# Ten of sixteen 256-column groups of the second block's first FFN product as seven products of half blocks

## The chip, the core and the metric

The kernel runs on one core of a Trainium2 chip. The metric is the device time of one execution in microseconds (us). One execution is also taken with the hardware profiler; its rows are what this text reads. Engines are named as in the profile: PE (TensorE, matmuls), PEld (its weight loads), DVE (VectorE), ACT (ScalarE), POOL (GpSimd) and SP (which only issues transfers here).

## What is computed

Two blocks of a transformer, each with two layers, on 512 tokens of 1024 features in float32. The change touches only the feed-forward part of the second block, twice (two layers):

```python
D_FF_2 = 4 * D_MODEL            # 4096, with D_MODEL = 1024 and 512 tokens

def second_block(x, ...):
    for l in range(DEPTH):      # DEPTH = 2
        ...                     # mixer: pooling and sparse attention
        h = rms_norm_2(x, g_pre_ffn[l])
        f = jnp.square(jax.nn.relu(h @ w_ff1[l])) @ w_ff2[l]
        x = x + rms_norm_2(f, g_post_ffn[l])
```

The first product is `h @ w_ff1[l]`: 512 x 1024 by 1024 x 4096.

## The kernel before, in words

**Float32 by three products.** Every weight and every activation that goes into a large product is split into a high part (type fp32r, tiles `wh`, `hh`) and the rest (`wl`, `hl`). `mm3` issues three matmuls, high by high, high by low, low by high, which add up in PSUM. ACT makes the high part of a weight tile of 128 x 1024 (L212) and DVE subtracts it for the low part (L214). The third matmul of `mm3` is the first that reads `wl`.

**Weights.** `specs` lists all weight tiles in the order of use. `prefetch_raw` issues their loads on SP into two buffers `wr`; `prefetch` splits them; `weights()` hands the next one out and keeps two split tiles (two buffers of `wh` and `wl`) ahead. `place_next` names another tile as the place of a coming split.

**The first FFN product, `ffn2`.** The hidden features come in eight groups g of 512 columns. A group takes four weight tiles (256 rows by 512 columns each), and of each tile 24 matmuls with 512 moving columns (tokens): 96 matmuls, into four PSUM tiles `mm`. The sums over the eight row blocks are kept with features on the partitions, four tiles of 128 x 512. When one is done, ACT writes its relu into `hq<g>` (L1631) and DVE squares it there (L1632). The normalisation's gain per feature is in `hh` and `hl` already; its factor per token is applied after the second product. In the last layer `last_tokens` (32 transposes of `x` on PE, eight copies on ACT) is woven into group 1. Then `out_ffn` or, in the last layer, `out_last` makes the second product.

**Half blocks elsewhere.** `gemm_feat_halves` already runs group 0 in halves of 256 tokens: its matmuls have 256 moving columns, with a weight load of 128 x 128 for each as everywhere.

**Order.** The program is written as generators; a scheduler then places the instructions on the engines, each of which runs its own queue in order.

Of the kernel before, what the change touches and what calls it, by code (L numbers as in the profile page):

```python
# [9 lines left out]
F32 = mybir.dt.float32  # L10
# [6 lines left out]
P = 128  # L17
# [74 lines left out]
class Net:  # L92
# [36 lines left out]
    def specs(self):  # L129
# [30 lines left out]
        for l in range(self.n2):  # L160
            w = a["w_in_2"][l]
            rows512(w, 2048, NK)
            small(w, 2560, 72)
            for c0 in (1024, 512, 1536):
                rows512(w, c0, NK)
            for f in range(4):
                out.append([(w[:, f * P:(f + 1) * P], 0, P, NK)])
            for g in range(2):
                rows512(a["w_out_2"][l], 512 * g, NK)
            for g in range(8):  # L170
                rows512(a["w_ff1_2"][l], 512 * g, NK)
            full(a["w_ff2_2"][l], 32)
        return out

    def start_weights(self):
        self.spec = self.specs()
# [3 lines left out]
    def prefetch_raw(self, n):  # L180
        nc = self.nc
        while self.n_raw < min(self.n_get + n, len(self.spec)):
            r = self.wp.tile([P, 1024], F32, name="wr", bufs=RAW)
            width = sum(s[2] for s in self.spec[self.n_raw])
            for src, c0, n, kk in self.spec[self.n_raw]:
                nc.sync.dma_start(r[:, :kk * width].rearrange("p (k c) -> p k c", k=kk)[:, :, c0:c0 + n],
                                  src.rearrange("(k p) c -> p k c", p=P))
            self.raw[self.n_raw] = (r, kk, width)
            self.n_raw += 1

    def prefetch(self, n):
# [1 line left out]
        self.prefetch_raw(n + 1)  # L193
        end = min(self.n_get + n, len(self.spec))
        while self.n_split < end:
            r, kk, width = self.raw.pop(self.n_split)
            n = kk * width
            if self.n_split in self.place:
                pool, name = self.place.pop(self.n_split)
# [16 lines left out]
            self.n_split += 1  # L216

    def weights(self):
        n = 2
        while self.n_get + n in self.place:  # L220
            n += 1
        self.prefetch(n)
        self.n_get += 1
        return self.split.pop(self.n_get - 1)
# [61 lines left out]
    def gemm_tok(self, pt, x, n):  # L286

        for i, (k, t) in enumerate(self.ends_apart(n)):
            if k % 2 == 0 and i % 8 == 0:
                wh, wl = self.weights()  # L290
            s = slice(t * P, (t + 1) * P)
            self.mm3(pt[t], x[k][0][:, s], x[k][1][:, s], wh[:, k % 2, :], wl[:, k % 2, :], k == 0, k == n - 1)
            if i % 4 == 3:
                yield

    def gemm_small(self, pt, x, m):
        wh, wl = self.weights()
# [668 lines left out]
    @staticmethod  # L966
    def four(t):
        return t.rearrange("p (a b) -> p a b", a=4)
# [646 lines left out]
    def ffn2(self, l):  # L1615
        nc, V, tc = self.nc, self.nc.vector, self.tc
        with tc.tile_pool(name=f"fg{l}", bufs=1, reuse_waits="tile") as pool:
            pts = yield from self.take_first()
            rcol = self.rcol
            r2 = pool.tile([P, NT], F32, name="rf2")  # L1620
            V.tensor_tensor(r2, rcol, rcol, op=OP.mult)
            hid = []
            last = l + 1 == self.n2
            fill = [self.last_tokens(pool, "g_post_ffn_2", l)] if last else []
            for g in range(8):
                if g:
                    pts = [self.mm() for _ in range(4)]
                    yield from self.weave(self.gemm_feat(pts, self.xs, NK), fill)
# [5 lines left out]
            if last:  # L1634
                yield from self.out_last(pool, hid, 32, r2)
            else:
                yield from self.out_ffn(pool, hid, 32, "g_post_ffn_2", l, r2,
                                        lambda n: pool.tile([P, S], F32, name="fsq", bufs=4),
                                        ("g_pre_mix_2", l + 1, True, True))

    def run(self):
        with self.tc.tile_pool(name="init", bufs=1) as self.init:
# [45 lines left out]
```

## Time and profile before

| what | value |
|---|---|
| time, median of 3 runs | 2646.94 us (2641.33 to 2652.8) |
| the profiled execution's own time | 2646.93 us |
| its span in the trace | 2645.2 us |
| PE busy | 2605.6 us, 99% of the span |
| DVE, ACT, POOL busy | 59%, 43%, 10% |
| granted TensorE clock | 0.995 of full speed over the span |

The profiled execution agrees with the median, so a sum made against its trace can be set beside the median. 1.7 us of its time lie outside the span. A busy share is a mean over all stages; what a stage is worth is read in that stage.

### The profile page before, as it was taken

The numbers are of one execution on the slowest core, as the hardware profiler recorded it, in microseconds if no ns is written. First come the engines' busy times: TensorE is split into PE (matmuls) and PEld (weight loads), VectorE is DVE, ScalarE is ACT, GpSimd is POOL, SyncE is SP. The second block draws the span as 40 slices with busy tenths as digits, with TensorE's granted clock in tenths as the row PEclk, the third lists the DMA queues.
The fourth block names the chain that finished last, engine by engine and source line by source line (L and its number), as shares of the span: only waits on it lengthen the run. The fifth ranks groups of instructions, "written<-read, shape, count | busy, mean of one in ns | idle before, by whom it ended". The sixth has DMA issues, their size and how long they took to land. (4 is left out here: it accounts for less than half of the span.)

```text
span 2645.2 us, 35427 instructions
## 1 busy us (share of the span) xinstructions
PE 2605.6 (99%) x13656; PEld 2113.5 (80%) x13656; DVE 1549.0 (59%) x3122; ACT 1126.3 (43%) x1916; POOL 264.9 (10%) x356
## 2 busy tenths in 40 slices
PE   8999999999999999999999999999999999999998
PEld 7877788888988869888888767988888766988887
DVE  6946576663586576666626695634326686633434
ACT  5346543342443474433424555323224556423322
POOL 2100100000220002000002431100002331100000
PEclk9999999999999999999999998999999999999999
DMA  5331212333333112233332212133333222133322
GB/s 159 94 89 49 80 46 91 95 96 97 96 82 108 49 33 80 87 90 94 97 106 72 79 48 88 49 93 90 96 96 91 70 72 64 57 96 96 90 94 96
DMA packets 155568, 221.83 MB, mean 84 GB/s; under 512 B 25759, under 2 KB 92039, under 8 KB 155399
## 3 DMA queue, kind: packets, MB, share of 16 engines
q1 hardware_dynamic: 154007, 216.92, 27.5%
q0 software_dynamic: 832, 2.63, 0.4%
q8 instruction: 107, 1.75, 0.3%
q14 instruction: 62, 0.51, 0.1%
q10 hardware_dynamic: 560, 0.01, 0.0%
HBM read 212.70 MB, written 6.83 MB: 83 GB/s over the span
## 5 line engine op out<-in xcount | busy, mean ns | idle before, releaser
L234 PE MATMUL mm<-hh,wh 128*128 128x512 f32 (+2 forms) x1924 | 740.5, 387 | 2.4 <-ACT wh L212 1.1
L214 DVE TENSOR_TENSOR wl<-wr,wh 128x1024 fp32r<-128x1024 f32 (+1 forms) x312 | 385.1, 1234 | 607.9 <-ACT wh L212 595.1
L235 PE MATMUL mm<-hl,wh 128*128 128x512 f32 (+2 forms) x1924 | 738.8, 384 | 0.0
L236 PE MATMUL mm<-hh,wl 128*128 128x512 f32 (+2 forms) x1924 | 734.7, 382 | 0.0
L212 ACT ACTIVATE wh<-wr 128x1024 fp32r<-128x1024 f32 (+1 forms) x336 | 354.0, 1055 | 730.6 <-PE mm L235 401.4
L234 PEld LDWEIGHTS mm<-hh,wh 128*128 128x128 f32 (+1 forms) x1924 | 362.9, 189 | 80.5 <-ACT wh L212 1.5
L236 PEld LDWEIGHTS mm<-hh,wl 128*128 128x128 f32 (+1 forms) x1924 | 361.5, 188 | 77.5
L235 PEld LDWEIGHTS mm<-hl,wh 128*128 128x128 f32 (+1 forms) x1924 | 362.0, 188 | 73.5 <-issue 0.3
L234 PE MATMUL mm<-wh,hh 128*128 128x512 f32 x524 | 213.9, 408 | 0.0
L236 PE MATMUL mm<-wh,hl 128*128 128x512 f32 x524 | 207.8, 397 | 0.0
L235 PE MATMUL mm<-wl,hh 128*128 128x512 f32 x524 | 207.8, 396 | 0.0
L234 PEld LDWEIGHTS mm<-wh,hh 128*128 128x128 f32 x524 | 98.6, 188 | 28.3 <-issue 4.9
L236 PEld LDWEIGHTS mm<-wh,hl 128*128 128x128 f32 x524 | 98.7, 188 | 23.7
L235 PEld LDWEIGHTS mm<-wl,hh 128*128 128x128 f32 x524 | 98.9, 189 | 20.9
L1269 DVE TENSOR_TENSOR hl<-hq,hh 128x512 fp32r<-128x512 f32 x92 | 63.0, 687 | 73.0 <-ACT hh L1268 72.9
L1382 ACT ACTIVATE fy<-fxc,par 128x512 f32<-128x512 f32 x88 | 67.1, 810 | 78.4 <-DVE fxc L1379 78.4
L1268 ACT ACTIVATE hh<-hq 128x512 fp32r<-128x512 f32 x92 | 57.2, 622 | 94.9 <-PE dx L235 78.8
L481 ACT ACTIVATE hh<-x,par 128x256 fp32r<-128x256 f32 x128 | 60.9, 504 | 72.5 <-DVE x L562 72.2
L736 PE MATMUL ax<-tb,v 128*64 128x128 f32 x640 | 71.2, 293 | 7.8 <-DVE tb L721 7.4
L736 PEld LDWEIGHTS ax<-tb,v 128*64 128x64 f32 x640 | 44.4, 139 | 42.0 <-DVE tb L721 16.8
L1379 DVE TENSOR_TENSOR fxc<-mm,rrep 128x512 f32<-128x512 f32 x88 | 60.0, 689 | 29.7 <-PE mm L236 25.4
L214 POOL TENSOR_TENSOR wl<-wr,wh 128x1024 fp32r<-128x1024 f32 x24 | 58.4, 2435 | 109.4 <-ACT wh L212 109.2
(666 smaller groups left out, 4466.3 us busy)
## 6 DMA issues: line engine op xcount, KB each, us to landing
wr<-in_w_ff_dram SPq DMA_DIRECT2D x128, 512.0 KB, 3.6
wr<-in_w_in_dram SPq DMA_DIRECT2D x96, 512.0 KB, 3.7
wr<-in_ffn_w_in_dram SPq DMA_DIRECT2D x176, 256.0 KB, 3.2
wr<-in_ffn_w_out_dram SPq DMA_DIRECT2D x44, 512.0 KB, 3.5
wr<-in_w_out_dram SPq DMA_DIRECT2D x32, 512.0 KB, 3.6
xt<-in_x_dram SPq DMA_DIRECT2D x4, 512.0 KB, 7.5
scm<-dM SPq DMA_DIRECT2D x2, 1024.0 KB, 4.5
out_dram<-hq SPq DMA_DIRECT2D x8, 256.0 KB, 2.0
```

The lines of the kernel that those rows point to most:

```text
L212: nc.scalar.activation(h[:, :n], r[:, :n], AF.Copy)
L214: eng.tensor_tensor(lo[:, :n], r[:, :n], h[:, :n].bitcast(F32), op=OP.subtract)
L234: t.matmul(out, ah, bh, start=first, stop=False, skip_group_check=shared)
L235: t.matmul(out, ah, bl, start=False, stop=False, skip_group_check=shared)
L236: t.matmul(out, al, bh, start=False, stop=last, skip_group_check=shared)
L481: nc.scalar.activation(self.hh[k][:, c], self.x[k][:, c], AF.Copy, scale=g)
L736: T.matmul(o[self.head_rows(e), h // 2 * P:(h // 2 + 1) * P], v[:, j, (h + e) * 64:(h + e + 1) * 64], pT[e][:, j * P:(j + 1) * P], start=j ...
L1268: nc.scalar.activation(h, hid[k], AF.Copy)
L1269: V.tensor_tensor(lo, hid[k], h.bitcast(F32), op=OP.subtract)
L1379: V.tensor_tensor(xc[:, 2:], pt, rrep, op=OP.mult)
L1382: nc.scalar.activation(y, xc[:, 2:], AF.Identity, scale=w(2), bias=self.pcol("ffn_conv_b", l, r))
```

## The change

Five of the eight groups of `ffn2` (g = 2 to 6, that is ten of sixteen groups of 256 columns) are computed by a scheme of seven products in place of eight. A group's weights are cut into four blocks of 512 rows by 256 columns (W11, W12, W21, W22; the first digit is the half of the columns, the second that of the rows), the activations into four blocks of 512 features by 256 tokens. Seven products of such blocks are made, four of them (S1, S2, S3, S4) with sums or differences of weight blocks, and four (S1, S2, S3, W22) with sums or differences of activation blocks. Each product is 24 matmuls with 256 moving columns.

- **Activations, once a layer (`seven_terms`, written ahead of group 1's product):** `x` is scaled again in float32 (four 128x512 scalings on ACT, four on DVE), four differences of 128x1024 are taken on DVE, and each is split (ACT high, DVE low). They live in tiles that are needed later (`hq5`, `hq6`, `hq7`, `w5`, and `ga`, `gb` or `xtok`).
- **Weights:** `load_block` loads a block of 128 x 4 x 256 (rows of 1 KB, where the tiles before had rows of 2 KB) into one of six slots (four in a tile `tail`, two in `wr`); `sum_block` makes S1 to S4 with one DVE operation of 128x1024 each, in place. Seven splits a group in place of four. `weights()` keeps three split tiles ahead, and every third goes into a tile `t4`.
- **Results (`seven_groups`):** one PSUM tile `ax` gathers W11, then S2, S3 and W22 on top of each other; W12 and S1 with S4 have two `mm` tiles. ACT keeps a copy of three stages, DVE adds three, and relu and square (both on ACT now) of a result are written one product later. The product W22 of a group is put behind the first product of the next group.
- `last_tokens` is woven into group 7, no longer into group 1; the scratch tile of the post-norm (`fsq`) becomes `t4`.

```diff
-                rows512(a["w_ff1_2"][l], 512 * g, NK)
+                if g not in self.SEVEN_GROUPS:
+                    rows512(a["w_ff1_2"][l], 512 * g, NK)
+                elif g == self.SEVEN_GROUPS[0]:
+                    out.extend((op, a["w_ff1_2"][l], 512 * h) for h, op in self.seven_order())
...
+    SEVEN = ("W11", "W12", "S1", "S2", "S4", "S3", "W22")
+    SEVEN_GROUPS = range(2, 7)
+    def seven_order(self):
+        gs, out = self.SEVEN_GROUPS, []
+        for g in gs:
+            ops = [(g, op) for op in self.SEVEN[:6]]
+            out += ops[:1] + [(g - 1, "W22")] * (g > gs[0]) + ops[1:]
+        return out + [(gs[-1], "W22")]
+    def load_block(self, op, w, c0):
+        if op == "W11":
+            self.blk.append({})
+        for b in {"W11": ("W11",), "W12": ("W12",), "S1": ("W21", "W22")}.get(op, ()):
+            f, k = int(b[1]) - 1, int(b[2]) - 1
+            t = self.blk[-1][b] = self.slots.pop(0)
+            self.nc.sync.dma_start(t.rearrange("p (k c) -> p k c", k=4),
+                                   w[k * 512:(k + 1) * 512, c0 + f * 256:c0 + (f + 1) * 256]
+                                   .rearrange("(k p) c -> p k c", p=P))
+    def sum_block(self, op):
+        b, V = self.blk[-1 if op == "W11" else 0], self.nc.vector
+        if op == "S1":
+            b["S"] = self.slots.pop(0)
+            V.tensor_tensor(b["S"], b["W21"], b["W22"], op=OP.add)
+        elif op == "S2":
+            V.tensor_tensor(b["S"], b["S"], b["W11"], op=OP.subtract)
+        elif op == "S4":
+            V.tensor_tensor(b["W12"], b["W12"], b["S"], op=OP.subtract)
+            self.slots += [b["S"], b["W12"]]
+        elif op == "S3":
+            V.tensor_tensor(b["W11"], b["W11"], b["W21"], op=OP.subtract)
+            self.slots += [b["W21"], b["W11"]]
+        elif op == "W22":
+            self.blk.pop(0)
+            self.slots.append(b["W22"])
+        return b[{"S1": "S", "S2": "S", "S4": "W12", "S3": "W11"}.get(op, op)]
 
...
+            if self.spec[self.n_raw][0] in self.SEVEN:
+                if self.n_raw >= self.n_get + 6 or len(self.slots) < 2:
+                    break
+                self.load_block(*self.spec[self.n_raw])
+                self.n_raw += 1
+                continue
...
-            r, kk, width = self.raw.pop(self.n_split)
+            if self.spec[self.n_split][0] in self.SEVEN:
+                r, kk, width = self.sum_block(self.spec[self.n_split][0]), 4, 256
+            else:
+                r, kk, width = self.raw.pop(self.n_split)
...
-        n = 2
+        n = 3 if self.spec[self.n_get][0] in self.SEVEN else 2
...
+    def seven_terms(self, y, ts, g):
+        nc, V = self.nc, self.nc.vector
+        four = lambda t: t.rearrange("p (k c) -> p k c", k=4)
+        for k in range(NK):
+            if k < 4:
+                nc.scalar.activation(y[0][:, k], self.x[k], AF.Copy, scale=g(k))
+            else:
+                V.tensor_scalar(y[1][:, k - 4], self.x[k], g(k), None, op0=OP.mult)
+        y11, y12, y21, y22 = [b[:, :, h * HALF:(h + 1) * HALF] for b in y for h in range(2)]
+        V.tensor_tensor(y11, y12, y11, op=OP.subtract)
+        V.tensor_tensor(y12, y22, y12, op=OP.subtract)
+        V.tensor_tensor(y22, y22, y11, op=OP.subtract)
+        V.tensor_tensor(y21, y21, y22, op=OP.subtract)
+        out = {}
+        for n, t, d in zip(("S1", "S2", "S3", "W22"), ts, (y11, y22, y12, y21)):
+            h, lo = out[n] = four(t[:, 0]), four(t[:, 1])
+            nc.scalar.activation(h, d, AF.Copy)
+            V.tensor_tensor(lo, d, h.bitcast(F32), op=OP.subtract)
+        for n, k, h in (("W11", 0, 0), ("W12", 4, 0), ("S4", 4, 1)):
+            out[n] = [t[:, k:k + 4, h * HALF:(h + 1) * HALF] for t in (self.hha, self.hla)]
+        return out
+    def seven_groups(self, pool, terms):
+        nc, V = self.nc, self.nc.vector
+        two = lambda p: p.rearrange("p (a b) -> p a b", a=2)
+        keep = lambda o, p: nc.scalar.activation(o, two(p), AF.Copy)
+        add = lambda o, p: V.tensor_tensor(o, two(p), o, op=OP.add)
+        st, late = {}, []
+        def end(o, src):
+            nc.scalar.activation(o, src, AF.Relu)
+            nc.scalar.activation(o, o, AF.Square)
+        for n, (g, op) in enumerate(self.seven_order()):
+            if op == "W11":
+                blk = pool.tile([P, 4, S], F32, name=f"hq{g}")
+                out = {(f, t): blk[:, 2 * f:2 * f + 2, t * HALF:(t + 1) * HALF] for f in range(2) for t in range(2)}
+                st[g] = dict(a=self.ax(), out=out, blk=blk)
+            s, out = st[g], st[g]["out"]
+            if op in ("W12", "S1"):
+                s[op] = self.mm()
+            pt = s[{"W12": "W12", "S1": "S1", "S4": "S1"}.get(op, "a")]
+            if n % 3 == 2:
+                self.place_next(3, pool, ("t4",))
+            wh, wl = self.weights()
+            h, lo = terms[op]
+            for f in range(2):
+                c, o = slice(f * P, (f + 1) * P), pt[:, f * HALF:(f + 1) * HALF]
+                for k in range(4):
+                    self.mm3(o, wh[:, k, c], wl[:, k, c], h[:, k], lo[:, k],
+                             op in ("W11", "W12", "S1") and f == 0 and k == 0, k == 3, True)
+            for o, src in late:
+                end(o, src)
+            late = []
+            where = {"W11": (0, 0), "W12": (0, 0), "S1": (1, 1), "S2": (0, 1), "S4": (0, 1), "S3": (1, 1), "W22": (1, 0)}
+            o = out[where[op]]
+            if op in ("W11", "S1", "S2"):
+                keep(o, pt)
+            elif op == "W22":
+                late.append((o, two(pt)))
+            else:
+                add(o, pt)
+                late.append((o, o))
+            yield
+        for o, src in late:
+            end(o, src)
+        self.seven_out = [st[g]["blk"][:, f] for g in self.SEVEN_GROUPS for f in range(4)]
 
...
+            self.slots = [t[:, i] for t in [pool.tile([P, 4, 1024], F32, name="tail")] for i in range(4)]
+            self.slots += [self.wp.tile([P, 1024], F32, name="wr", bufs=RAW) for _ in range(2)]
+            self.blk = []
             for g in range(8):
+                if g == 1:
+                    y = [pool.tile([P, 4, S], F32, name=n) for n in ("hq5", "hq6")]
+                    if last:
+                        t = pool.tile([P, 4, 1024], F32R, name="xtok")
+                        ts = [t[:, 0:2], t[:, 2:4]]
+                    else:
+                        ts = [pool.tile([P, 2, 1024], F32R, name=n) for n in ("ga", "gb")]
+                    ts += [pool.tile([P, 2, 1024], F32R, name=n) for n in ("w5", "hq7")]
+                    terms = self.seven_terms(y, ts, lambda k: self.pcol("g_pre_ffn_2", l, k))
+                if g == self.SEVEN_GROUPS[0]:
+                    yield from self.seven_groups(pool, terms)
+                    hid += self.seven_out
+                if g in self.SEVEN_GROUPS:
+                    continue
+                if last and g == 7:
+                    fill.append(self.last_tokens(pool, "g_post_ffn_2", l))
```

The rows below are the scheduler's order, before and now, at two places. In the rows of the changed program the helpers have new line numbers: L269 is the DVE's low part of a weight split, L207, L209, L211 and L214 are the block sums S1, S2, S4 and S3, L361 the scalings, L363 to L366 the differences and L371 the low parts of the activation terms, L382 an addition of a product to its result, L1786 the square.

DVE, from the end of the normalisation's statistics in the first layer to the weights of group 1, before (`wl` are the third and fourth tiles of group 1 and the first of group 2):

```order
L1621 TENSOR_TENSOR rf2_15056<-rcol_14883 128x4
L548 TENSOR_TENSOR f2_16999<-rf2_15056 128x2
L548 TENSOR_TENSOR f2_17142<-rf2_15056 128x2
L1632 TENSOR_TENSOR hq0_15058<-hq0_15058 128x512 x4
L214 TENSOR_TENSOR wl_15100<-wr_12375,wh_15099 128x1024
L214 TENSOR_TENSOR wl_15128<-wr_12377,wh_15127 128x1024
L214 TENSOR_TENSOR wl_15156<-wr_12379,wh_15155 128x1024
```

The same place now:

```order
L361 TENSOR_SCALAR hq6_14949<-x_77,par_84 128x512 x2
L676 TENSOR_TENSOR f2_17518<-rf2_14934 128x2
L676 TENSOR_TENSOR f2_17656<-rf2_14934 128x2
L363 TENSOR_TENSOR hq5_14948<-hq5_14948 128x4x256
L364 TENSOR_TENSOR hq5_14948<-hq6_14949,hq5_14948 128x4x256
L371 TENSOR_TENSOR ga_14950<-hq5_14948,ga_14950 128x1024
L365 TENSOR_TENSOR hq6_14949<-hq6_14949,hq5_14948 128x4x256
L371 TENSOR_TENSOR w5_14952<-hq5_14948,w5_14952 128x1024
L366 TENSOR_TENSOR hq6_14949<-hq6_14949 128x4x256
L371 TENSOR_TENSOR gb_14951<-hq6_14949,gb_14951 128x1024
L269 TENSOR_TENSOR wl_15007<-wr_12375,wh_15006 128x1024
L371 TENSOR_TENSOR hq7_14953<-hq6_14949,hq7_14953 128x1024
```

Seven operations of 128x1024 now stand between the squares of group 0 and the low part of group 1's third tile (`wr_12375` in both).

DVE within the seven groups, one whole group from its W12 to the first product of the next (tile `hq4` is group 4; `t4`, `wl` are the three places of split weights):

```order
L269 TENSOR_TENSOR wl_15518<-tail_14936,wh_15517 128x1024
L269 TENSOR_TENSOR wl_15550<-wr_14938,wh_15549 128x1024
L209 TENSOR_TENSOR wr_14938<-wr_14938,tail_14936 128x1024
L211 TENSOR_TENSOR tail_14936<-tail_14936,wr_14938 128x1024
L269 TENSOR_TENSOR t4_15554<-wr_14938,t4_15554 128x1024
L214 TENSOR_TENSOR tail_14936<-tail_14936,wr_14937 128x1024
L382 TENSOR_TENSOR hq4_15513<-mm_15581,hq4_15513 128x2x256
L269 TENSOR_TENSOR wl_15612<-tail_14936,wh_15611 128x1024
L269 TENSOR_TENSOR wl_15645<-tail_14936,wh_15644 128x1024
L207 TENSOR_TENSOR tail_14936<-tail_14936,wr_14937 128x1024
L269 TENSOR_TENSOR t4_15648<-tail_14936,t4_15648 128x1024
L382 TENSOR_TENSOR hq4_15513<-mm_15609,hq4_15513 128x2x256
```

Before, a group was four rows of L214 and four squares; now its sums, splits and additions share one queue, the four sums mostly ahead of the splits that need them, and the sum S1 of group 5 (L207) stands ahead of group 5's first split.

PE at the end of the seven groups in the first layer (`w5` is the term of S3, `hq7` that of W22, `mm_16348` begins group 7):

```order
L291 MATMUL ax_15959<-w5_14952,wl_16083 128x256
L289 MATMUL mm_16348<-hh_78,t4_16261 128x512
L290 MATMUL mm_16348<-hl_79,t4_16261 128x512
L291 MATMUL mm_16348<-hh_78,t4_16261 128x512
L289 MATMUL mm_16349<-hh_78,t4_16261 128x512
L289 MATMUL ax_15959<-hq7_14953,wh_16257 128x256
```

Four matmuls of group 7 have been moved between the last S3 and the last W22, which add into the same PSUM tile.

## Rows read from the trace of the kernel before

**Rows 1.** The page: span, busy engines, the chain that ended last.
```profile
span 2645.2 us, 35427 instructions
...
PE 2605.6 (99%) x13656; PEld 2113.5 (80%) x13656; DVE 1549.0 (59%) x3122; ACT 1126.3 (43%) x1916; POOL 264.9 (10%) x356
...
PE 38%; DVE 5%; POOL 1%; ACT 1%; issue 0%; DVEq 0%; ACTq 0%; POOLq 0%
```

**Rows 2.** Busy time by stretch: five groups, by layer; columns as named.
```profile
core 0: us, PE busy (x) PEld busy (x) DVE busy (x) ACT busy (x) POOL busy (x), PEclk, DMA share, GB/s
1713.42:1825.42 112.00, 112.00 (x482) 90.09 (x480) 37.66 (x41) 32.58 (x41) 0.00 (x0) 1.00 0.32 94
2320.95:2432.95 112.00, 112.00 (x481) 90.09 (x481) 37.64 (x40) 32.62 (x41) 0.00 (x0) 1.00 0.32 94
```

**Rows 3.** PE in order of time: start us, duration; 512 columns, then 256.
```profile
1702.22 0.40 PE L234 MATMUL mm<-hh,wh 128*128 128x512 f32 x1
...
1710.62 0.40 PE L234 MATMUL mm<-hh,wh 128*128 128x512 f32 x1
...
1672.10 0.28 PE L235 MATMUL mm<-hl,qs 128*128 128x256 f32 x1
...
1681.82 0.29 PE L235 MATMUL mm<-hl,wh 128*128 128x256 f32 x1
```

**Rows 4.** Busy time in a stretch of 256 columns, and in one group.
```profile
1672.00:1681.60 9.60, 9.60 (x83) 9.60 (x82) 9.40 (x21) 4.33 (x9) 3.52 (x4) 1.00 0.00 0
...
1713.42:1735.82 22.40, 22.40 (x98) 18.02 (x96) 7.53 (x9) 6.52 (x9) 0.00 (x0) 1.00 0.33 94
```

**Rows 5.** Groups of instructions, DVE and ACT: xcount, busy us, mean ns, idle before.
```profile
L214 DVE TENSOR_TENSOR wl<-wr,wh 128x1024 fp32r<-128x1024 f32 x20 | 24.5, 1225 | 67.3 <-ACT wh L212 67.3
...
L493 DVE TENSOR_TENSOR iqT<-iqT,qT 128x1024 f32<-128x1024 f32 x1 | 1.2, 1219 | 0.0
...
L1379 DVE TENSOR_TENSOR fxc<-mm,rrep 128x512 f32<-128x512 f32 x88 | 60.0, 689 | 29.7 <-PE mm L236 25.4 <-ACT rrep L516 4.0
...
L212 ACT ACTIVATE wh<-wr 128x1024 fp32r<-128x1024 f32 x21 | 22.2, 1059 | 69.1 <-PE mm L235 69.1
L1631 ACT ACTIVATE hq<-mm 128x512 f32<-128x512 f32 x20 | 11.9, 594 | 10.9 <-PE mm L236 10.9
...
L1268 ACT ACTIVATE hh<-hq 128x512 fp32r<-128x512 f32 x92 | 57.2, 622 | 94.9 <-PE dx L235 78.8 <-PE mm L236 16.0
```

**Rows 6.** ACT in order of time at groups 0 and 1, first layer.
```profile
1691.22 0.60 ACT L1631 ACTIVATE hq<-mm 128x512 f32<-128x512 f32 x1 [0.84 <-PE mm L236]
1696.58 1.06 ACT L212 ACTIVATE wh<-wr 128x1024 fp32r<-128x1024 f32 x1 [4.77 <-PE mm L235]
1702.18 1.06 ACT L212 ACTIVATE wh<-wr 128x1024 fp32r<-128x1024 f32 x1 [4.54 <-PE mm L235]
```

**Rows 7.** DVE in order of time, same place.
```profile
1697.68 1.22 DVE L214 TENSOR_TENSOR wl<-wr,wh 128x1024 fp32r<-128x1024 f32 x1 [5.13 <-ACT wh L212]
...
1708.88 1.23 DVE L214 TENSOR_TENSOR wl<-wr,wh 128x1024 fp32r<-128x1024 f32 x1 [4.37 <-ACT wh L212]
1710.05 0.70 DVE L1632 TENSOR_TENSOR hq<-hq 128x512 f32<-128x512 f32 x1
```

**Rows 8.** ACT operations of 128x512 with a parameter column: ns min/median/max.
```profile
L908 ACT ACTIVATE tb<-xc,par x8: 722/724/729, 167.5 to 891.0; 128x512 f32<-128x512 f32 x8
```

**Rows 9.** The transfers of weights: one line's landing, and DMA by stretch.
```profile
DMA to landing us min/median/max: 2.8/3.6/8.2
...
wr<-in_ffn_w_in_dram SPq DMA_DIRECT2D x82, 256.0 KB, 3.1
...
310.00:560.00 250.00, 249.27 (x1278) 209.96 (x1277) 164.16 (x262) 100.52 (x133) 19.84 (x53) 1.00 0.29 87
```

**Rows 10.** ACT in order of time, group 1 of the last layer.
```profile
2303.87 1.06 ACT L212 ACTIVATE wh<-wr 128x1024 fp32r<-128x1024 f32 x1 [1.99 <-PE mm L235]
...
2317.70 1.06 ACT L212 ACTIVATE wh<-wr 128x1024 fp32r<-128x1024 f32 x1 [4.44 <-PE mm L235]
```

More of the change, by code (lines that the diff above doesn't have):

```diff
@@ L1619, in ffn2, with sq @@
             rcol = self.rcol
+            sqs = []
+            def sq(n):
+                if not sqs:
+                    sqs.append(pool.tile([P, 4, S], F32, name="t4"))
+                return sqs[0][:, n % 4]
             r2 = pool.tile([P, NT], F32, name="rf2")
@@ L1623, in ffn2 @@
             last = l + 1 == self.n2
-            fill = [self.last_tokens(pool, "g_post_ffn_2", l)] if last else []
+            fill = []
+            self.slots = [t[:, i] for t in [pool.tile([P, 4, 1024], F32, name="tail")] for i in range(4)]
+            self.slots += [self.wp.tile([P, 1024], F32, name="wr", bufs=RAW) for _ in range(2)]
+            self.blk = []
             for g in range(8):
+                if g == 1:
[14 more added lines that the diff above has]
+                    fill.append(self.last_tokens(pool, "g_post_ffn_2", l))
                 if g:
@@ L1637, in ffn2 @@
                 yield from self.out_ffn(pool, hid, 32, "g_post_ffn_2", l, r2,
-                                        lambda n: pool.tile([P, S], F32, name="fsq", bufs=4),
-                                        ("g_pre_mix_2", l + 1, True, True))
+                                        sq, ("g_pre_mix_2", l + 1, True, True))
     def run(self):
```

## Prediction

> **What bounds the kernel now.** I read the page first: PE is busy 99% of the span, and in the chain that ended last nothing but PE has a large share, with almost no issue time [rows 1]. So I ask what PE's time is made of in the stage that changes, and whether the other engines have room. The busy time by stretch answers both: five groups of the first FFN product take 112.00 us in either layer, PE is busy in all of it at full granted clock, DVE in 37.7 us and ACT in 32.6 [rows 2]. The stage is a stream of matmuls and nothing else; only fewer or shorter matmuls can shorten it, and DVE and ACT have two thirds of their time to give.
>
> What a matmul costs is not its recorded duration (they overlap) but the distance of starts. With 512 moving columns, 36 matmuls start between 1702.22 and 1710.62: 8.40 / 36 = 0.2333 us. With 256 columns, 81 start between 1672.10 and 1681.82: 9.72 / 81 = 0.1200 us, though DVE was busy in nearly all of that stretch [rows 3, 4]. Half the columns cost 51.4%, not 50%.
>
> **The matmuls.** Before, a group is 96 matmuls: 96 x 0.2333 = 22.4 us, which the stretch of one group confirms [rows 4]. Now it is 7 products x 24 = 168 of 256 columns: 168 x 0.1200 = 20.16 us. That is 2.24 us a group, 11.2 us for five, **22.4 us** in two layers. It is the whole gain, and it comes only where PE never waits.
>
> **A rule against it.** The Trainium skill, "TensorE: Matmul & The Clock Gate", section "Back-to-back issue gap", gives for a stream of weight load and matmul about 81 ns at 128 columns and 131 ns at 512; between them, 256 columns would be about 98 ns (an estimate from that page). By it a group would go from 12.6 to 16.4 us, and the change would cost some 38 us. The trace does not agree: 120 and 233 ns here.
>
> **DVE's and ACT's load in a group.** DVE before: four low parts at 1.225 and four squares. Now: seven low parts (8.6 us), four block sums at 1.22 (4.9), three additions from PSUM at 0.69 (2.1): 15.6 us of 20.16. ACT: seven high parts at 1.06 (7.4), three copies at 0.59 (1.8), eight of relu and square at 0.62 (5.0): 14.2 us [rows 5]. Both fit, 77% and 70%; the question is the order in which they stand.
>
> **Inside the groups.** I lay one group out by the order of the rows, with T = 0 at the start of its first product and a product every 2.88 us. A split can begin when the product three places back has been read, and must be done when its own starts, so it has 5.76 us; it needs 1.06 + 1.23. W12's low part is done at 2.5, S1's at 5.4. The sums S2 and S4 follow to 7.9, S2's low part to 9.2 (wanted at 11.5), the sum S3 to 10.4, the addition of W12 to 11.1, S4's low part to 12.3 (wanted at 14.4). S3's high part stands on ACT behind relu and square of that addition and a copy, so its low part ends near 15.2 (wanted at 17.3). Then comes the next group's sum S1, which needs both blocks W21 and W22 of that group. The later of them goes into a slot that is free only after S4's low part, at 12.3, and lands 3.6 us later (the median of the transfers) [rows 9], at about 16. So DVE stands a little, the sum ends at 17.3, the next W11's low part at 18.5 (wanted at 20.2), the addition of S3, for which the last W22 waits, at 21.2 (wanted at 23.0). The tightest slack is 1.8 us. I take **0** for the inside. Rows of 1 KB in place of 2 KB cost nothing that I can see: block 1's FFN loads 1 KB rows at 87 GB/s with a DMA share of 0.29, this stage 94 GB/s with 0.32 [rows 2, 9], the same share for a byte.
>
> **The way in, once a layer.** Before, ACT's last relu of group 0 starts at 1691.22; the third weight tile of group 1 is first read at 1702.22, its low part by the third matmul at 1702.69; the split itself needs only the matmuls of two tiles back [rows 3, 6, 7]. Now ACT scales x four times behind that relu, at 0.72 each [rows 8], in a queue some 0.1 less: until about 1694.4. DVE's first difference waits for it, and then seven operations of 128x1024 and the third tile's low part follow, each leaning on the one ahead. Back to back such an operation takes 1.17 (1708.88 to 1710.05 [rows 7]); with small waits I take 1.2: 8 x 1.2 = 9.6, so the low part is there at 1704.0, and PE waits 1.4 us. Bounds: scalings like plain copies (0.59) and 1.17 give 0.5; scalings at 0.8 and 1.3 an operation give 2.7. After that, W11 and W12 are split in time, but the first group's third product frees nothing early: S1's low part, the sum S2, the addition of W12, the sum S4 and S2's low part stand in a row on DVE behind the end of the first product, and S2's low part comes some 0.6 us after the matmul that wants it (0 to 1.5). Together **2.0 us a layer** (0.5 to 4.2), 4.0 in two. The rest of that work (four scalings, the last low part) lies beside the matmuls of group 1, whose cover is the 67 us that DVE stood idle in five groups [rows 5].
>
> **The way out.** The last W22 adds into the tile that DVE must first read for the last S3. Four matmuls of group 7 stand between, 4 x 0.233 = 0.93 us; the addition needs 0.69 and the way of its signals. I take 0.2 a layer (0 to 1): **0.4**. The transposes of the last layer cost group 1 about 13.83 - 11.2 = 2.6 us between two of its splits [rows 10]; in group 7 the same instructions stand beside the same kind of matmuls: 0 (plus or minus 2.6). The squares that go from DVE to ACT are in the loads above. `t4` for `fsq` changes no order on the path: 0.
>
> **The sum.** 2646.93 - 22.4 + 4.0 + 0.4 = 2628.9, against the profiled execution's own time, which is the median of the runs. I predict **2629 us**, 0.68% less; about 0.5%, 13 us, is what a measurement of this kernel can tell from no change.
>
> **Rivals.**
> *The blocks come late.* The sum S1 stands at the head of DVE's queue and waits for a transfer; everything behind it, splits, additions, waits too. For it: the slot is freed late in the group, and the slowest transfer took 8.2 us [rows 9]. Against it: the median is 3.6, and 1.8 us of slack. From a landing of about 5.4 us on, each further microsecond costs one in each of four groups of a layer, 8 us in all. At 6.8 us it is 11 us: 2640. The way in at its upper bound (4 us more) ends near the same.
> *DVE runs in series* (the other side). If DVE stands before each of the seven low parts for its own high part (1.06 and a signal, 1.1) because the sums don't fill those gaps, a group takes 15.6 + 7.7 = 23.3 us, and with 1.2 us of standing for a transfer 24.5, against 22.4 before: 2.1 us a group, 21 us, 2668. It decides from 6.8 us of standing a group, more than six of the seven; to be slower by more than 0.5% it takes 8.1. Against it: the order puts most sums and additions into just those gaps, and in my layout DVE stands 4.6 us.
> *Weight loads set the pace.* Loads were busy 9.60 of 9.60 us in the short stretch, 18.02 of 22.40 in the long one [rows 4]. If 168 loads took what 96 took there, 0.188 us each, a group would be 31.5 us, 91 us more in all: 2738. (By the skill's page above the change also loses, though by less.) But 80 loads did go through in 9.6 us.
>
> **How the numbers follow.** Forecast 0.65, by its own bounds 2622 to 2636; late blocks or a dear way in 0.22, 2636 to 2648; series 0.11, 2648 to 2670; loads 0.02. Faster by over 0.5% is nearly all of the forecast and a little of the second: 0.65. Slower is most of the series and the loads: 0.10. The rest, 0.25, is the same. The range goes from all waits at nothing (2646.9 - 22.4, and 0.2% of spread) to a gain wholly lost: 2619 to 2648.
>
> **What would show it.** Matmuls 0.120 us apart inside groups 2 to 6, and 20.2 us from one group's first product to the next's; PE idle of about 1.4 us ahead of the third tile of group 1, released by DVE's low part, and of some 0.6 in the first S2; DVE near 77% busy and ACT near 70% in the groups. Wrong would be: a matmul distance over 0.125; PE idle in every group, and if so, DVE's block sum behind a transfer (late blocks) or DVE's low parts behind ACT with no sum in the gap (series); a landing of blocks over 5 us; PE idle in group 7 of the last layer behind copies of the transposes.

## The result, and the profile after

The changed kernel takes 2624.61 us (median of 9 executions, 2617.86 to 2641.07) against 2645.93 (9 executions) before: a ratio of 0.993, interval 0.9905 to 0.9954. That is 21 us and 0.7% faster (12 to 25 us by the interval). The forecast was 2629.

The page of its profiled execution (2618.65 us), against [rows 1]:

```profile
span 2616.9 us, 37121 instructions
...
PE 2573.4 (98%) x14376; PEld 2125.0 (81%) x14376; DVE 1645.4 (63%) x3206; ACT 1205.7 (46%) x2032; POOL 266.5 (10%) x356
...
PE 35%; DVE 6%; ACT 1%; POOL 1%; issue 1%; DMA 0%; DVEq 0%; ACTq 0%; POOLq 0%
```

PE still sets the time, DVE has gained 4 points. The two profiled spans differ by 28.3 us, 7 more than the medians, and the difference must not all be put down to the change: the stage begins 6 us earlier already, behind code that is the same in both. Busy time by stretch (clock third from the right) in the mixer ahead of it, before:

```profile
1570.00:1590.00 20.00, 19.36 (x105) 11.04 (x103) 19.43 (x57) 15.29 (x38) 4.52 (x6) 1.00 0.00 1
1590.00:1610.00 20.00, 18.04 (x90) 11.18 (x91) 12.30 (x34) 11.63 (x27) 0.00 (x0) 0.66 0.08 27
```

and after, about the same place of the program:

```profile
1585.00:1605.00 20.00, 17.59 (x116) 10.68 (x116) 16.68 (x47) 15.81 (x38) 0.00 (x0) 1.00 0.09 27
```

In the execution of before the granted clock fell to a mean of 0.66, part of the stretch at the lower level (1.2 GHz), while PE had gaps and waited for DVE; in that of after it did not fall there. Every profile of this study has such dips, mostly at gaps of the mixers, here in one execution and there in another. In the stage that changes the clock is 1.00 in both, so I compare the stage by itself.

From the last matmul of group 0 to the first of the second product (PE in order of time) the stage took 1690.90 to 1847.82 and 2297.27 to 2457.73 before, 1684.79 to 1832.20 and 2280.88 to 2429.45 after: 156.92 and 160.46 us against 147.41 and 148.57. That is 9.5 and 11.9 us, **21.4 in all**, where the prediction has 18.0 (22.4 less 4.4), and it agrees with the difference of the medians, 21.3.

The five groups with the first four matmuls of group 7, by layer, against [rows 2]:

```profile
1708.42:1810.72 102.30, 100.40 (x846) 99.41 (x844) 75.14 (x72) 66.91 (x90) 0.00 (x0) 1.00 0.30 94
2304.57:2405.34 100.77, 100.29 (x846) 99.42 (x844) 75.22 (x72) 68.06 (x92) 0.00 (x0) 1.00 0.31 95
```

Less 4 x 0.233 for those four, the groups take 101.4 and 99.8 us instead of 112.0. DVE is busy 73 to 75% of it, ACT 65 to 68%; 77 and 70 were forecast. What PE waited for in the first layer's stage (us in total, times, longest):

```profile
PE ax L291 <- DVE wl L269: 1.7, 2, 1.2
PE mm L289 <- ACT hq L1785: 0.7, 1, 0.7
PE mm L289 <- ACT hq L381: 0.2, 1, 0.2
```

and in the second's: only `PE ax L291 <- DVE wl L269: 0.5, 1, 0.5`. Counted by the gaps (in the point on waits below) all waits come to 4.6 us where 4.4 were forecast, but they are not where they were forecast.

**The matmuls** were quicker. PE in order of time, first and last of the 24 of three products, hh with `wh`, hh with `t4`, and the term `ga` with `wh`:

```profile
1726.21 0.29 PE L289 MATMUL ax<-hh,wh 128*128 128x256 f32 x1
...
1728.97 0.28 PE L291 MATMUL ax<-hh,wl 128*128 128x256 f32 x1
...
1731.92 0.28 PE L289 MATMUL mm<-hh,t 128*128 128x256 f32 x1
...
1734.62 0.28 PE L291 MATMUL mm<-hh,t 128*128 128x256 f32 x1
1734.73 0.28 PE L289 MATMUL mm<-ga,wh 128*128 128x256 f32 x1
...
1737.34 0.28 PE L291 MATMUL mm<-ga,wl 128*128 128x256 f32 x1
```

2.76 / 23 = 0.1200, 2.70 / 23 = 0.1174 and 2.61 / 23 = 0.1135 us: the distance that the prediction read [rows 3] does not hold for every product. The waits that show inside the groups of the first layer are gaps of 0.85, 1.43 and 0.45 us, 2.37 over the common distance; 101.4 - 2.4 = 99.0 for 840 matmuls is 0.1179 each.

**The entry.** Group 0's relus, and PE around them:

```profile
1684.79 0.28 PE L291 MATMUL mm<-hh,ta 128*128 128x256 f32 x1
...
1685.11 2.07 ACT L1785 ACTIVATE hq<-mm 128x512 f32<-128x512 f32 x4 [6.36 <-PE mm L291]
1685.76 0.50 PE L289 MATMUL mm<-hh,wh 128*128 128x512 f32 x1 [0.69 <-ACT hq L1785]
...
1687.04 2.57 ACT L359 ACTIVATE hq<-x,par 128x512 f32<-128x512 f32 x4
```

Before, the four relus stood 1.4 us apart, the last at 1691.22 [rows 6], each behind its own tile. Now all four wait for the very last matmul, and group 1, which needs the PSUM tile that a relu frees, begins 0.85 us later than it could.

**The third tile of group 1**, where 1.4 us were forecast:

```profile
1697.06 0.39 PE L289 MATMUL mm<-hh,wh 128*128 128x512 f32 x1
1697.29 0.40 PE L290 MATMUL mm<-hl,wh 128*128 128x512 f32 x1
1697.53 0.39 PE L289 MATMUL mm<-hh,wh 128*128 128x512 f32 x1
...
1697.72 1.22 DVE L269 TENSOR_TENSOR wl<-wr,wh 128x1024 fp32r<-128x1024 f32 x1
...
1698.69 0.40 PE L290 MATMUL mm<-hl,wh 128*128 128x512 f32 x1
1698.99 0.50 PE L291 MATMUL mm<-hh,wl 128*128 128x512 f32 x1
```

The low part does come late, at 1698.94, but the scheduler has put eight matmuls that need only the high part ahead of the first that needs it, and PE hardly stands.

**A late block.** SyncE's queue, DVE and PE at group 4 in the first layer:

```profile
1736.90 1.22 DVE L269 TENSOR_TENSOR t<-wr,t 128x1024 fp32r<-128x1024 f32 x1
...
1738.15 0.37 SPq L198 DMA_DIRECT2D wr<-in_w_ff_dram  x1
...
1744.85 1.23 DVE L207 TENSOR_TENSOR wr<-wr,tail 128x1024 f32<-128x1024 f32 x1 [4.99 <-DMA wr<-in_w_ff_dram]
...
1747.27 0.39 PE L291 MATMUL ax<-hh,wl 128*128 128x256 f32 x1 [1.15 <-DVE wl L269]
```

The load starts when S4's low part (1736.90 + 1.22) has freed its place, as laid out, and lands 6.6 us later. The prediction let PE wait from a landing of 5.4 us on: 6.6 - 5.4 = 1.2, and 1.15 is what PE waited. The load is the third of three that go out within 2.3 us (1735.88, 1737.01, 1738.15); loads with none just ahead of them landed in 3.6 to 4.0 us in this stage. In the second layer the same load is issued at 2334.22 and read at 2339.78, 5.6 us on, and PE hardly waits.

### The profile page after: what moved, and what is told of

Read it like the earlier page. It is cut to its first block, busy times and chain, and to the rows that moved or that the text cites. A ratio compares the mean times of both kernels' runs of the same rounds, so it can differ in the third digit from the quotient of the medians.

```text
span 2616.9 us, 37121 instructions
## 1 busy us (share of the span) xinstructions
PE 2573.4 (98%) x14376; PEld 2125.0 (81%) x14376; DVE 1645.4 (63%) x3206; ACT 1205.7 (46%) x2032; POOL 266.5 (10%) x356
## 5 line engine op out<-in xcount | busy, mean ns | idle before, releaser
L289 PE MATMUL mm<-hh,wh 128*128 128x512 f32 (+2 forms) x1684 | 633.7, 378 | 3.3 <-ACT wh L267 1.1
L269 DVE TENSOR_TENSOR wl<-wr,wh 128x1024 fp32r<-128x1024 f32 (+1 forms) x286 | 353.7, 1237 | 447.5 <-ACT wh L267 443.8
L290 PE MATMUL mm<-hl,wh 128*128 128x512 f32 (+2 forms) x1684 | 633.2, 376 | 0.0
L291 PE MATMUL mm<-hh,wl 128*128 128x512 f32 (+2 forms) x1684 | 627.1, 374 | 0.0
L267 ACT ACTIVATE wh<-wr 128x1024 fp32r<-128x1024 f32 (+1 forms) x310 | 326.4, 1054 | 587.3 <-PE mm L290 242.3
L289 PEld LDWEIGHTS mm<-hh,wh 128*128 128x128 f32 (+1 forms) x1684 | 317.2, 188 | 68.0 <-ACT wh L267 1.5
L291 PEld LDWEIGHTS mm<-hh,wl 128*128 128x128 f32 (+1 forms) x1684 | 315.6, 188 | 62.3 <-DVE wl L269 0.6
L290 PEld LDWEIGHTS mm<-hl,wh 128*128 128x128 f32 (+1 forms) x1684 | 315.9, 188 | 57.4 <-issue 0.3
L291 PE MATMUL mm<-wh,hl 128*128 128x512 f32 x524 | 207.8, 397 | 0.0
L289 PEld LDWEIGHTS mm<-wh,hh 128*128 128x128 f32 x524 | 98.7, 188 | 28.3 <-issue 4.9
L291 PEld LDWEIGHTS mm<-wh,hl 128*128 128x128 f32 x524 | 98.7, 188 | 23.6
L269 POOL TENSOR_TENSOR wl<-wr,wh 128x1024 fp32r<-128x1024 f32 x24 | 58.4, 2432 | 111.4 <-ACT wh L267 111.2
```

Of the source, the lines that this page charges most:

```text
L267: nc.scalar.activation(h[:, :n], r[:, :n], AF.Copy)
L269: eng.tensor_tensor(lo[:, :n], r[:, :n], h[:, :n].bitcast(F32), op=OP.subtract)
L289: t.matmul(out, ah, bh, start=first, stop=False, skip_group_check=shared)
L290: t.matmul(out, ah, bl, start=False, stop=False, skip_group_check=shared)
L291: t.matmul(out, al, bh, start=False, stop=last, skip_group_check=shared)
```

## The experiments

Each was compared with executions of the kernel before on its own chip, so ratios are set against ratios: 0.993 for the change itself. One hundredth of a ratio is 26 us.

**1. Half the columns, nothing saved** (kernel before).

```
-  self.mm3(pt[f], wh[:, j % 2, s], wl[:, j % 2, s], x[k][0], x[k][1], ...)
+  for t in range(2):      # groups 2 to 6
+      c = slice(t * HALF, (t + 1) * HALF)
+      self.mm3(pt[f][:, c], wh[:, k % 2, s], wl[:, k % 2, s], x[k][0][:, c], x[k][1][:, c], ...)
```

> The kernel before, with groups 2 to 6 of block 2's first FFN product done in 256-column halves: 192 matmuls a group instead of 96 of 512 columns, no block sums, no terms, nothing saved. Theory (a 256-column matmul costs about 0.118 us here, whatever else runs): a group takes 192 x 0.118 = 22.6 us, five groups 113.1, and the time is about 2 us over the kernel before, 2648. The prediction's own distance of 0.120 gives 23.0 a group and 2652. Rival (DVE and ACT hold the changed kernel's matmuls up, and PE alone would be quicker): the distance falls to 0.1135, the pace of the quickest products of the changed kernel, and a group takes 21.8 us, 2640.

Ratio 1.0027 (1.0012 to 1.0043), 7 us slower. The five groups by stretch:

```profile
1713.07:1828.27 115.20, 115.20 (x962) 115.19 (x960) 37.52 (x41) 32.62 (x40) 0.00 (x0) 1.00 0.32 92
```

115.20 / 960 = 0.1200: the prediction's own distance, not 0.118. So 0.1200 is right for hh with `wh`, `wl`, and the rival falls: with DVE idle two thirds of the time the matmuls are not quicker than in the changed kernel but slower. What made those quicker stays open here (experiments 8 to 11 and the last section).

**2. One group instead of five.**

```
-    SEVEN_GROUPS = range(2, 7)
+    SEVEN_GROUPS = range(2, 3)
```

> The changed kernel with one group (2) in seven products and groups 3 to 6 as before. Theory (the gain is 2.6 us for each group that is in seven products, less about 1.8 us of waits once a layer on the way in): 2 x (2.6 - 1.8) = 1.6 us faster than before, 2644. Rival (most of the gain is something that comes with the change but not with the number of groups, the clock or the new order at the entry): most of the 21 us stays, 2626 to 2630. Rival of the prediction's own sizes: 2 x (2.24 - 2.2) = 0, 2646.

Ratio 0.9993 (0.9977 to 1.001). The stages took 156.32 and 159.13 us, 1.9 less than before together, where 1.6 was expected. The fixed price of the way in eats what one group saves; the gain comes from the number of groups.

**3. The tile for blocks allocated later.**

```
-            self.slots = [t[:, i] for t in [pool.tile([P, 4, 1024], F32, name="tail")] for i in range(4)]
...
                 blk = pool.tile([P, 4, S], F32, name=f"hq{g}")
+                if g == 0:
+                    self.slots = [t[:, i] for t in [pool.tile([P, 4, 1024], F32, name="tail")] for i in range(4)]
...
```

> The changed kernel with the 16 KB tile for the blocks allocated after group 0's output instead of before it; no operation added or removed. Theory (the output of group 0 lay on memory that the matmuls of group 0 still read as weights, so its four relus waited for the last of them): the relus start one by one again, PE's wait of 0.7 us ahead of group 1 in the first layer goes, the stage of the first layer is 146.4 us instead of 147.3; the second layer gains less, as transposes stand there. In all 1 us, too little for the time to show. Rival (the scheduler's order, not the memory, puts the relus together): nothing changes, 147.3.

The order of the instructions is the same on PE, DVE and ACT. ACT in order of time:

```profile
1685.52 0.60 ACT L1786 ACTIVATE hq<-mm 128x512 f32<-128x512 f32 x1 [2.18 <-PE mm L291]
1686.83 0.60 ACT L1786 ACTIVATE hq<-mm 128x512 f32<-128x512 f32 x1 [0.70 <-PE mm L291]
...
1689.71 0.60 ACT L1786 ACTIVATE hq<-mm 128x512 f32<-128x512 f32 x1 [0.84 <-PE mm L291]
```

The relus stand apart again and PE goes on at once (last matmul of group 0 at 1689.39, group 1 at 1689.51). The stages: 145.42 and 148.42 us, 2.0 and 0.1 less; 0.85 of the first is this wait, the rest mostly a shorter wait for the late block (0.5 instead of 1.2). In the changed kernel `hq0` lies at bytes 126464 to 134656 of a partition and overlaps `ta` and `qs` of the pool before it (120384 to 136768), which group 0's matmuls read to the end; in the kernel before it lay at 110080 to 118272, clear of both. The memory is shown to be the cause. The whole time, 0.9908 (0.989 to 0.9925), can't tell 2 us.

**4. Two places for split weights.**

```
-        n = 3 if self.spec[self.n_get][0] in self.SEVEN else 2
+        n = 2
...
-            if n % 3 == 2:
-                self.place_next(3, pool, ("t4",))
```

> The changed kernel with two places for split weights instead of three: a split may begin only when the product two places back has been read, and has 2.88 us instead of 5.76. Theory (the third place is what lets DVE do sums and additions while ACT makes the next high part): DVE falls into series, 15.6 + 7 x 1.1 = 23.3 us a group, 3.1 us a group over the changed kernel, 2656, and no gain is left. Rival (DVE at 70% has slack enough, the place is not needed): 2625 to 2630.

Ratio 1.0 (0.9986 to 1.0015): no gain is left. PE's waits in the first layer's stage:

```profile
PE ax L291 <- DVE wl L269: 8.2, 9, 1.4
PE ax L289 <- DVE hq L382: 0.9, 1, 0.9
```

Nine waits for low parts: at S2 of every group and at W11 of every group but the first. The stages are 8.6 and 11.1 us longer than the changed kernel's, 2 us a group where 3.1 were expected, and in the second some 1.7 us of it are TensorE's clock, which was granted at 0.57 from 2369 to 2373, behind one of the waits. DVE, busy 73.9 of 110.0 us in the first layer, falls only partly into series. The expected price was half as large again as the measured one.

**5. The sum S1 three times.**

```
-            V.tensor_tensor(b["S"], b["W21"], b["W22"], op=OP.add)
+            for _ in range(3):
+                V.tensor_tensor(b["S"], b["W21"], b["W22"], op=OP.add)
```

> The changed kernel with the block sum S1 done three times over in each group: 2 x 1.22 = 2.4 us more on DVE a group, nothing else. Theory (the prediction's layout of a group: the tightest slack on DVE is 1.8 us): each further microsecond over 1.8 costs one, 0.6 us in each of ten groups, 6 us, 2630. Rival (DVE in series is already at its limit, so each microsecond on DVE costs one): 24 us, 2649. Rival (DVE's idle time in a group, 30% of 20 us, is all usable): no change, 2625.

Ratio 0.9963 (0.995 to 0.9976), 9 us slower than the changed kernel by ratios whose intervals just touch; the stages 2.5 and 6.0 us longer, 8.5 in all. Waits in the second layer's stage:

```profile
PE ax L290 <- DVE hq L383: 4.1, 2, 3.0
PE ax L292 <- DVE wl L270: 0.5, 1, 0.5
```

The place is the one of the layout: the addition of S3, for which the last W22 waits. The size is not shown so well. In the mean it is 0.85 a group of the 2.44 added, as if the slack were 1.6 us, where 1.8 was laid out; but PE stood at five of the eight W22s between two groups, 1.1 to 3.2 us, and not at the others. The longest wait stands behind a block sum that itself waited 3.1 us for its transfer, and behind that wait the granted clock fell to 0.65 in the mean, so that 24 matmuls took 4.2 us instead of 2.9:

```profile
2363.50:2367.60 4.10, 4.10 (x24) 4.10 (x25) 2.98 (x3) 2.67 (x4) 0.00 (x0) 0.65 0.28 96
```

That about two thirds of the 24 us added to DVE cost nothing is shown; a slack for each group is not.

**6. W22 right behind S3.**

```
-            out += ops[:1] + [(g - 1, "W22")] * (g > gs[0]) + ops[1:]
+            out += [(g, op) for op in self.SEVEN]
...
```

> The changed kernel with each group's seventh product W22 right behind S3 instead of behind the first product of the next group. Both add into the same PSUM tile, and DVE must read it in between. Theory (what the interleaving hides is the addition and its signals): PE stands about 1.0 us ahead of each W22, as the changed kernel with two places did once in a layer, 10 us in all, 2635. If the addition also stands behind a block sum of 1.2 us in DVE's queue, twice as much, 2647. Rival (the interleaving is not needed): 2625.

Ratio 0.9974 (0.9957 to 0.9992); the stages 7.0 and 4.9 us longer, 11.9 in all. The size is near, the place is not. PE and DVE in order of time:

```profile
1753.25 0.28 PE L289 MATMUL ax<-hl,t 128*128 128x256 f32 x1
...
1753.65 1.23 DVE L206 TENSOR_TENSOR wr<-wr,tail 128x1024 f32<-128x1024 f32 x1 [3.67 <-DMA tail<-in_w_ff_dram]
...
1756.67 0.39 PE L290 MATMUL ax<-hh,t 128*128 128x256 f32 x1 [3.14 <-DVE t L268]
...
1757.49 0.28 PE L288 MATMUL ax<-hq,wh 128*128 128x256 f32 x1
```

The scheduler pulled eight matmuls of the next group's W11 ahead of W22 to cover the addition, and it is W11's low part that is missing: it stands behind the next group's S1, and that behind a transfer. What the interleaving buys is time for the blocks of the next group. Some 1.6 of the 11.9 us are TensorE's clock again, 0.60 in the mean behind the wait shown:

```profile
1757.50:1761.80 4.30, 4.30 (x26) 4.30 (x25) 1.23 (x1) 1.41 (x3) 0.00 (x0) 0.60 0.00 0
```

**7. One more place for blocks, first layer only.**

```
+            self.slots += [] if last else [pool.tile([P, 1024], F32, name="wr3")]
```

> The changed kernel with one more place of 4 KB for raw blocks in the first layer (the second has no room for it and stays as it is, a control). Theory (a block of group 4 lands late, 6.6 us after its issue, because its place came free late; that is the prediction's rival of late blocks, in one group only): PE's waits of 1.2 and 0.2 us in groups 4 and 5 of the first layer go, its stage is 145.8 us instead of 147.3, the second layer's stays 148.3. Rival (the transfer itself is slow there): the waits stay.

Stages 144.88 and 148.31: 2.5 us less in the first layer, 0.3 in the second. PE waits in the first only 0.6 us, at the first S2; the waits in groups 4 and 5 are gone, and DVE's for a transfer there is 1.80 us instead of 4.99. So the wait came from the places and not from a transfer that is slow by itself: with one place more the loads of groups 3 to 5 go out 1.3 us apart or more instead of three within 2.3 us, and those whose landing is recorded take 3.7 to 4.7 us. The 4 KB also moved `hq0`, and group 1 begins 0.25 us behind group 0 instead of 0.97, so 0.7 of the 2.5 belongs to experiment 3. Ratio 0.9934 (0.9914 to 0.9954), no difference in the whole time.

**8 to 11. Where the operands begin.** Two unused tiles; 8 (`align64`) has both, 9 (`pad_ahead`) the first, 10 (`pad_behind`) the second, 11 (`before_align64`) both in the kernel before.

```
+        self.const.tile([P, 8], F32, name="pad1")
         self.hha = self.const.tile([P, NK, S], F32R, name="hh")
         self.hla = self.const.tile([P, NK, S], F32R, name="hl")
+        self.const.tile([P, 8], F32, name="pad2")
```

> The changed kernel with two unused tiles of 32 bytes a partition, one ahead of the activations hh and hl, one behind them: hh, hl then begin at a multiple of 64 bytes (before: 32 beside one), all later tiles 64 bytes further. No operation added. In the changed kernel a 256-column matmul takes 0.120 us from the next when both operands lie in the lower tiles (hh with wh and wl) and 0.113 to 0.118 when one of them lies in the pool of the stage. Theory (where the operands begin in memory sets this distance): 0.113 to 0.118 now for hh with wh and wl too; the 512-column distance of 0.2333 either falls with it (then up to 3% of the whole kernel, 2550) or not (then 3 to 10 us, 2615 to 2622). Rival (it is something else about these tiles, such as both parts lying in one tile): nothing changes, 2625.

> The changed kernel with only the first of the two unused 32-byte tiles: hh and hl begin at a multiple of 64 bytes, the weight tiles wh and wl and all later tiles 32 bytes beside one. With both tiles (hh, hl, wh, wl all at multiples of 64) the time was 2607 us, with none (hh and hl 32 beside, wh and wl at multiples) 2625. Theory (the moving operand's beginning alone counts): like both, 2607. Rival (both operands must begin at a multiple of 64): like none, 2625, or slower.

> The changed kernel with only the second of the two unused tiles: hh and hl stay 32 bytes beside a multiple of 64, wh and wl come to lie 32 beside one as well, so both operands begin at the same remainder. Theory (the moving operand alone counts) and rival (both must begin at a multiple of 64): 2625 or slower. Second rival (the two must only have the same remainder): 2607.

> The kernel before with the two unused 32-byte tiles (hh, hl, wh, wl at multiples of 64 bytes). Theory (a matter of addresses that has nothing to do with the change): it gains as much as the changed kernel did, 17 to 22 us, 2624 to 2629, and the change is still worth about 20 us beside it. Rival (the gain needs the changed kernel's half blocks): no gain, 2645.

PE in order of time in group 1, 36 starts of 512 columns, `pad_ahead`:

```profile
1690.01 0.40 PE L292 MATMUL mm<-hh,wl 128*128 128x512 f32 x1
...
1698.17 0.40 PE L291 MATMUL mm<-hl,wh 128*128 128x512 f32 x1
```

and `pad_behind`:

```profile
1690.20 0.39 PE L292 MATMUL mm<-hh,wl 128*128 128x512 f32 x1
...
1698.22 0.39 PE L291 MATMUL mm<-hl,wh 128*128 128x512 f32 x1
```

8.16 / 35 = 0.2331 and 8.02 / 35 = 0.2291 us. All of them, with the bytes by which the tiles begin beside a multiple of 64 (from the program's allocation):

| kernel | hh, hl | wh, wl | 512 columns, this stage | 256, hh with wh, wl, this stage | ratio to before |
|---|---|---|---|---|---|
| changed | 32 | 0 | 0.2333 | 0.1200 | 0.9930 (0.9905 to 0.9954) |
| `pad_ahead` | 0 | 32 | 0.2333 | 0.1200 | 0.9903 (0.9874 to 0.9932) |
| `align64` | 0 | 0 | 0.2290 | 0.1178 | 0.9863 (0.9844 to 0.9882) |
| `pad_behind` | 32 | 32 | 0.2290 | 0.1178 | 0.9848 (0.9818 to 0.9877) |
| before | 32 | 0 | 0.2333 | 0.1200 | 1 |
| `before_align64` | 0 | 0 | 0.2289 | 0.1178 | 0.9922 (0.9897 to 0.9947) |

The order of instructions is the same in the changed kernel, `align64`, `pad_ahead` and `pad_behind`. The second rival of `pad_behind` holds for these tiles in this stage: not a multiple of 64 counts but the same remainder. It has nothing to do with the change: before gains 0.8% by it, and the change is worth 0.6 to 0.7% beside it still (0.9863 and 0.9848 against 0.9922; 16.8 and 15.9 us by the two stages).

The same remainder is not enough for the quick pace, though. PE in `align64`, in the first block of the network, with the same hh, hl, wh and wl in one stream without a gap:

```profile
1079.98 0.40 PE L293 MATMUL mm<-hh,wl 128*128 128x512 f32 x1
...
1086.16 0.39 PE L293 MATMUL mm<-hh,wl 128*128 128x512 f32 x1
...
1090.34 0.40 PE L293 MATMUL mm<-hh,wl 128*128 128x512 f32 x1
...
1096.63 0.40 PE L293 MATMUL mm<-hh,wl 128*128 128x512 f32 x1
```

6.18 / 27 = 0.2289 us, then 6.29 / 27 = 0.2330, and so it stays to the end of that product, near 1380. The granted clock is 1.00 on both sides of the change, at 1088; what set it off is not shown. `pad_behind` and `before_align64` change over in mid-stream too, near 458 us.

**12. Three edits together:** 3, 7 and 8.

> The changed kernel with the three edits that took a wait or a distance away: the tile for blocks allocated behind group 0's output, one more place for blocks in the first layer, the two unused 32-byte tiles. Theory (they add up): 2607 less 0.9 for the relus and less 1.5 for the late block, 2605. Rival (the moved addresses of the stage's pool cost what the waits gave): 2607 to 2610.

Ratio 0.9853 (0.9826 to 0.988), 2608.72 us: faster than both kernels, and not to be told from 8 or 10. The first layer's stage is the shortest of all, 143.68 us; the second's 148.10. The two stages together are 2.9 us shorter than in `align64`, where 2.4 were expected, so here the waits' gains add up. The rest of the kernel can hide that: in its profiled execution 2160 of some 3800 matmuls of hh with wh, wl at 512 columns (counted in blocks of 24) ran at 0.2333 us, in that of `align64` 1440; 720 x 0.0044 = 3.2 us (an estimate).

## Why the prediction was right, point by point

- **The matmuls** (forecast -22.4 us): mechanism right, size too small. 99.0 us a layer instead of 100.8 makes it -26.0. The step that was off is the price of a 256-column matmul, read from hh with its own weights and put on all seven products. Experiment 1 shows 0.1200 for that pair; in the changed kernel the products took 0.1133 to 0.1200, 0.1179 in the mean of all.
- **The rule against it** (the Trainium skill, "TensorE: Matmul & The Clock Gate", "Back-to-back issue gap") does not hold here: 0.113 to 0.120 us at 256 columns and 0.229 to 0.234 at 512 in every kernel run.
- **Waits** (forecast 4.0 in, 0.4 out, 0 inside): 3.5 in the first layer, which is 0.85 at the entry, 0.26 in group 1, 0.73 at the first S2, 1.3 and 0.3 in groups 4 and 5; some 1.1 in the second, together 4.6. The step "the third tile's low part is there late, and PE waits 1.4 us" failed: the low part is late, but the order gave PE eight other matmuls. The first S2 was forecast at 0.6 and took 0.5 by its releaser, 0.7 by the gap. The relus' wait (0.85) and the late block (1.3) were not foreseen at their places; that the total agrees is luck.
- **Inside the groups** (forecast 0): the order of the layout held, and with it the tightest place. The place of the late block came free 11.9 us into the group (12.3 laid out), and PE waited about from the landing laid out (5.4 us). What failed is the landing itself, taken at the median of 3.6 us for every load: one of them took 6.6. The slack of 1.8 us is not shown group by group (experiment 5).
- **The rivals.** Late blocks came once, 1.2 us, by the mechanism given. Series did not come; experiment 4 shows the third place to be what keeps DVE's low parts ahead of PE. The weight loads' price of 0.188 us did not come: no product took more than 0.120 a matmul outside the waits. They were busy 99.4 of 102.3 us, and that they have no part in the distance is not shown.
- **The way out** (forecast 0.4) **and the moved transposes** (forecast 0): nothing to be seen of either. PE went from S3 over four matmuls to W22 with no gap, and the second layer's other groups lost 0.3 us in all.

## What to carry to other kernels

Half the columns for an eighth fewer products paid here with DVE and ACT idle two thirds of the time before, and with a third place that lets a split begin two products early; without that place the whole gain was gone. A new tile at the head of a pool moves all the tiles behind it, and a first write may come to lie on memory that the stage before still reads: compare addresses, not only the order. Read a matmul's distance for each pair of operands that the change uses, and at more than one place, for the same pair ran at two paces.

## What the runs showed of the hardware that I had not expected

The distance of back-to-back matmuls depends on where their two operands begin in memory. An unused tile of 32 bytes (`pad_behind`), with the same instructions in the same order, took it from 0.2333 to 0.2290 us at 512 columns and from 0.1200 to 0.1178 at 256 in this stage, and the kernel from 0.993 to 0.985. The Trainium skill ("SBUF — State Buffer", "Operand start alignment") asks only for a multiple of the element size and says of its own measurements, none of them on TensorE, that they are "about legality, not speed"; the runs here add a speed.

What sets it is not settled. For hh and hl with wh and wl, the same remainder to 64 bytes allows the quicker pace (both ways: 0 and 0, 32 and 32), and at different remainders their long products at 512 columns stayed at 0.2333. But in the changed kernel `t4` and the terms begin at the same remainder, and their products took 0.119 to 0.120, slower than hh with `t4` (0.1175) at different ones.

Nor can the addresses of a product's own operands be all of it. The term `ga`, with `wh` at byte 81984 and `wl` at 90176 both times, took 0.1136 us a matmul in group 2 and 0.1178 in group 4 of the first layer, and `align64` changed its pace in the middle of a stream. So what ran before must count as well; no run here tells what it is.
